# Block products with seven instead of eight multiplications: seven more pairs, one weight sum made earlier, and a new order inside a piece by eight

## The chip, the cores and the metric

The kernel runs on one core of a Trainium2 chip. The metric is device time in microseconds of one execution, as the median of several runs. Lower is better. PE is TensorE (matmul), DVE is VectorE, ACT is ScalarE, POOL is GpSimd, SP is SyncE, which here only issues DMAs.

## The reference, cut to what matters

One encoder layer for 256 tokens with 2048 features, all in float32:

```python
h = rms_norm(x, attn_norm)
qa, ka, va, qb, kb, vb, ga, gb = split(h @ w_in)
ya = windowed_gqa(qa, ka, va, table, sink_a)
yb = dilated_attention(qb, kb, vb, table)
merged = sigmoid(ga) * (ya @ w_branch_a) + sigmoid(gb) * (yb @ w_branch_b)
x = x + merged @ w_out
hf = rms_norm(x, ffn_norm)
g = dwconv_centred(hf @ w_ffn_gate, conv_w, conv_b)
x = x + (gelu(g) * (hf @ w_ffn_up)) @ w_ffn_down
x = x + sigmoid(rms_norm(x, ple_norm) @ w_ple_gate) * (p @ w_ple_proj)
out = rms_norm(x, final_norm)
```

Nearly all of the work is the product of 256 tokens with each weight matrix. What the change touches are the products of `ga` and `gb` (the gate columns of `w_in`), of `w_out`, and of the second half of `w_ffn_down`.

## The kernel before, in words

**Pieces.** The weights lie in memory as a list of pieces of 128 x 2048 floats, in the order in which they are used; `_pieces` makes the list. Each piece is loaded by SP into one of three buffers `raw`. A float32 product is made of three passes: ScalarE copies a stretch of `raw` to a rounded high half (`uh`, L305), VectorE subtracts it from the original for the low half (`ul`, L306), and TensorE multiplies high by high, high by low and low by high (`thirds`). A converted stretch is a unit. Units of plain weights go into a ring of six buffers (`u`), units that hold sums of weights into a ring of two (`v`, named `vh` and `vl`). A unit is made when a buffer of its ring is free, strictly in the order of the list (`produce`, `pump`, `drop`).

**Pairs by eight and by seven.** In the stages that `quads` describes, a piece is a pair: two chunks of 128 input features for two blocks of 512 output columns. With the two halves of the 256 tokens these are 2 x 2 x 2 = 8 block products, each three matmuls of 512 columns. A letter says how the pair is multiplied. "s" makes the eight products. "S" and "Z" make seven, after Strassen and Winograd, from sums of weight blocks and sums of activation blocks. The sums of activations (`combine`, `sums_of`) are made once for a pair of chunks and used by all stages that share these activations. For "S" VectorE makes the weight sums in `raw` by three subtractions (L295 to L297: 1024, 512 and 512 columns). For "Z" one sum is made earlier and lies in memory, so two subtractions are left (L282, L283: 512 and 1024 columns), and `load` takes that quarter of the piece from there (L255). Either kind converts four units: 512 columns and 1024 of plain weights, and 1024 and 1024 of sums.

**Sums made earlier.** `sum_ahead` makes the early sum of a "Z" pair in two parts: POOL loads 128 x 3 x 256 floats (L268), VectorE makes two subtractions or additions of 256 columns (L271, L272), POOL stores 128 x 256 floats (L275). These steps use `keep`, so they stay in the order in which they are written. Before the change this is done only in the two gate and up stages of the MLP, one part a job, in two small buffers (`act2`, `S4`) in turn; with `LASTS` = 30, from job 30 on only at every second job.

**Stages.** A: the projections for attention, one head's columns a job (16 chunks), with the heads' attention laid in between: scores on PE, softmax on VectorE and ScalarE, transposes on PE, values on PE, each at an entry of the table `due` (`at`, `run_due`). `hb` holds the position biases. B0 to B3: a quarter of the columns of both gates, eight pairs each, and after each the two branch products (ba, bb), which are plain. D0, D1: the output projection, eight pairs each, 1024 columns. E0: gate and up for half of the MLP; F00, F01: the down projection of this half, eleven pairs each. E1, F10, F11: the same for the other half. Then pp0, pp1 and G0 to G3 for the last block. The patterns of letters are `ALT`, `FIRST_GATES` and `DOWN` (L95 to L99). The order of the work on each engine is set by the order in which the code is written together with a scheduler that may bring an instruction forward.

**Order in a piece by eight.** In `quad_stage` the eight products of an "s" pair run over token half, column block and chunk, the chunk innermost (`t, n, c = g // 4, g // 2 % 2, g % 2`), and both units are dropped at the end of the pair.

Of the kernel before, what the change touches and what calls it, by code (L numbers as in the profile page):

```python
# [112 lines left out]
def _pieces():  # L113
# [44 lines left out]
    quads("G0", ("w_ple_gate", 0), ("w_ple_gate", WIDE), ALT.replace("S", "Z"))  # L158
# [35 lines left out]
def _encoder(ctx: ExitStack, tc, xt, pt, xrow, cols, gainrow, table, onehot, mask, ident_in, wts, out):  # L194
# [89 lines left out]

    def produce():

        u = state["unit"]
        p, kind, a, b = _UNITS[u]
        while state["raw"] < min(p + 3, _NPIECES):
            load(state["raw"])  # L290
        raw = raws[p]
        ring = "u" if kind == "n" else "v"
        if kind == "T13":
            q = [raw[:, i * WIDE:(i + 1) * WIDE] for i in range(4)]
            nc.vector.tensor_tensor(raw[:, :2 * WIDE], raw[:, WIDE:3 * WIDE], raw[:, :2 * WIDE], op=ALU.subtract)  # L295
            nc.vector.tensor_tensor(q[2], q[2], q[0], op=ALU.subtract)
            nc.vector.tensor_tensor(q[3], q[3], q[2], op=ALU.subtract)  # L297
# [7 lines left out]
        nc.scalar.activation(hi, src, AF.Copy)  # L305
        nc.vector.tensor_tensor(lo, src, hi.bitcast(F32), op=ALU.subtract)  # L306
# [108 lines left out]
    def quad_stage(stage, moving, combos=None, tags=("M2", "M3", "M4", "P22")):  # L415
# [24 lines left out]
        for i, p in enumerate(pieces):  # L440
# [407 lines left out]

    for i, job in enumerate(_JOBS):
# [60 lines left out]
    def sums_of(u, tag, s=None):  # L910
# [8 lines left out]
        if s is None:  # L919
            s = tok.tile([P, 2, 4, P], FR, name="S", tag="S%d" % tag)  # L920
# [387 lines left out]
```

## Time and profile before

| | |
|---|---|
| median of 3 runs | 1455.45 us (1454.93 to 1456.0) |
| span of the profiled execution | 1453.7 us, 1.75 us under the median |
| instructions | 19747 |
| busy PE / DVE / ACT / POOL | 1442.7 / 1220.8 / 829.6 / 73.8 us |
| share of the chain that ended last | PE 98% |
| conversions on VectorE (L306) | 519 and 96 |
| mean DMA rate | 213 GB/s |
| stage A from 60 us / B0 / D0 / D1 / E0 | to 304.2 / from 304.2 / 541.7 / 583.7 / 627.5 us |
| stage E1 / F10 / F11 | from 986.8 / 1231.7 / 1288.1 us, F11 to 1346.0 |

The profile shows one execution. A row of the timeline gives start, length, engine, line, operation and, in brackets, the idle time before it with what ended it. Lengths overlap: an instruction may start before the one ahead of it on its engine has ended, so what an instruction costs in a full engine is the distance between two starts. A window's row gives the busy time of each engine in that stretch, with overlaps counted once.

### The profile page before, as it was taken

How to read it: one execution, taken by the hardware profiler on the slowest of the kernel's cores; microseconds unless marked ns; L12 is line 12 of the kernel's file. 1: busy time of each engine (PE TensorE's matmuls, PEld its weight loads, DVE VectorE, ACT ScalarE, POOL GpSimd, SP SyncE). 2: the span in 40 equal slices, each digit the busy share in tenths (PEclk: the TensorE clock that was granted, in tenths of full speed). 3: DMA queues.
4: the chain of work that ended last, by engine and by line, in shares of the span. 5: the costliest groups of instructions: out<-in, count | busy, mean ns of one | idle time of the engine just before them, and what ended most of it. 6: DMA issues, size and time to landing. Idle time of an engine off the chain costs nothing.

```text
span 1453.7 us, 19747 instructions
## 1 busy us (share of the span) xinstructions
PE 1442.7 (99%) x7470; PEld 1234.0 (85%) x7470; DVE 1220.8 (84%) x1730; ACT 829.6 (57%) x1148; POOL 73.8 (5%) x113
## 2 busy tenths in 40 slices
PE   9999999999999999999999999999999999999997
PEld 8888888888888888888888888888888888888885
DVE  7677665679998989989877999997878799998994
ACT  7455544546555656566545566465545466555753
POOL 0000000000000000000221100000121200000000
PEclk9999999999999999999999999999999999999998
DMA  9753445435456456465767655566776765556462
GB/s 330 252 209 146 155 167 175 172 143 203 189 190 231 180 210 239 178 253 203 277 238 267 241 208 198 189 248 227 263 275 243 271 236 213 197 194 233 173 236 82
DMA packets 58522, 310.17 MB, mean 213 GB/s; under 512 B 7028, under 2 KB 12020, under 8 KB 29500
## 3 DMA queue, kind: packets, MB, share of 16 engines
q1 hardware_dynamic: 49388, 280.46, 53.1%
q0 software_dynamic: 8320, 27.27, 5.2%
q8 instruction: 58, 0.95, 0.3%
q10 hardware_dynamic: 720, 1.19, 0.2%
q14 instruction: 36, 0.29, 0.1%
HBM read 299.94 MB, written 8.95 MB: 212 GB/s over the span
## 4 chain that ended last, share of the span: by engine, by line
PE 98%; DMA 0%; issue 0%; DVE 0%; ACT 0%; SPq 0%; POOLq 0%; POOL 0%; DVEq 0%
PE bank L351 29%; PE bank L358 15%; PE bank L408 15%; PE bank L409 14%; PE bank L410 14%; PE bank L397 2%; PE bank L399 2%; PE bank L398 2%; PE bank L335 2%; PE bank L336 1%; PE bank L939 1%; PE bank L755 0%; PE bank L703 0%; PE bank L702 0%; PE bank L701 0%; DMA raw<-in_wts 0%
## 5 line engine op out<-in xcount | busy, mean ns | idle before, releaser
L305 ACT ACTIVATE uh<-raw 128x1024 fp32r<-128x1024 f32 (+2 forms) x519 | 518.1, 1010 | 297.0 <-PE bank L410 106.5
L306 DVE TENSOR_TENSOR ul<-raw,uh 128x1024 fp32r<-128x1024 f32 (+2 forms) x519 | 594.4, 1164 | 96.5 <-ACT uh L305 65.9
L351 PE MATMUL bank<-hf,uh 128*128 128x512 f32 x1408 | 336.3, 391 | 0.0
L351 PEld LDWEIGHTS bank<-hf,uh 128*128 128x128 f32 x1408 | 258.9, 188 | 50.1
L358 PEld LDWEIGHTS bank<-hf,ul 128*128 128x128 f32 x1408 | 180.4, 191 | 6.7
L358 PE MATMUL bank<-hf,ul 128*128 128x256 f32 x1408 | 182.8, 283 | 0.0
L305 ACT ACTIVATE vh<-raw 128x1024 fp32r<-128x1024 f32 x96 | 101.1, 1058 | 59.8 <-DVE raw L282 27.0
L306 DVE TENSOR_TENSOR vl<-raw,vh 128x1024 fp32r<-128x1024 f32 x96 | 116.3, 1220 | 1.1
L351 PE MATMUL bank<-hs,uh 128*128 128x512 f32 x432 | 103.6, 392 | 0.0
L351 PEld LDWEIGHTS bank<-hs,uh 128*128 128x128 f32 x432 | 79.5, 188 | 15.6
L410 PE MATMUL bank<-uh,act 128*128 128x512 f32 x218 | 84.9, 390 | 0.0
L409 PE MATMUL bank<-ul,act 128*128 128x512 f32 x218 | 84.8, 389 | 0.0
L408 PE MATMUL bank<-uh,act 128*128 128x512 f32 x218 | 84.6, 390 | 0.0
L496 ACT ACTIVATE t<-bank 128x256 f32<-128x256 f32 x122 | 45.3, 374 | 59.8 <-PE bank L358 48.7
L408 PE MATMUL bank<-uh,hs 128*128 128x512 f32 x172 | 67.4, 392 | 0.0
L410 PE MATMUL bank<-uh,hs 128*128 128x512 f32 x172 | 67.2, 391 | 0.0
L409 PE MATMUL bank<-ul,hs 128*128 128x512 f32 x172 | 67.0, 389 | 0.0
L1084 ACT ACTIVATE gw<-gw,cl 128x256 f32<-128x256 f32 x44 | 24.0, 594 | 72.2 <-DVE gw L1081 71.9
L271 DVE TENSOR_TENSOR ahead<-ahead 128x256 f32<-128x256 f32 x52 | 21.9, 422 | 46.8 <-DMA ahead<-in_wts 46.8
L268 POOL DMA_DIRECT2D ahead<-in_wts x52 | 39.0, 750 | 375.7 <-DMA ahead<-ahead 207.0
L358 PE MATMUL bank<-hs,ul 128*128 128x256 f32 x432 | 56.6, 284 | 0.0
L358 PEld LDWEIGHTS bank<-hs,ul 128*128 128x128 f32 x432 | 54.5, 191 | 1.0
(266 smaller groups left out, 2423.8 us busy)
## 6 DMA issues: line engine op xcount, KB each, us to landing
raw<-in_wts SPq DMA_DIRECT2D x225, 1024.0 KB, 4.9
ahead<-in_wts POOLq DMA_DIRECT2D x52, 384.0 KB, 5.2
raw<-in_wts SPq DMA_DIRECT2D x26, 768.0 KB, 5.1
ahead<-ahead POOLq DMA_DIRECT2D x52, 128.0 KB, 4.4
raw<-ahead SPq DMA_DIRECT2D x26, 256.0 KB, 4.9
raw<-in_wts SPq DMA_DIRECT2D x12, 512.0 KB, 7.0
xr<-in_xrow SPq DMA_DIRECT2D x4, 512.0 KB, 8.4
x<-in_xt SPq DMA_DIRECT2D x13, 128.0 KB, 6.0
```

What stands on the lines that cost most here:

```text
L268: keep(nc.gpsimd.dma_start(q, wts[p][:, :3 * WIDE].rearrange("p (q c) -> p q c", c=WIDE)[:, :, cols]))
L305: nc.scalar.activation(hi, src, AF.Copy)
L306: nc.vector.tensor_tensor(lo, src, hi.bitcast(F32), op=ALU.subtract)
L335: nc.tensor.matmul(acc, hi[:, w], m, start=first, stop=False, skip_group_check=True)
L351: nc.tensor.matmul(acc, weights(u)[0][:, o * P:(o + 1) * P], m, start=first, stop=False, skip_group_check=True)
L358: nc.tensor.matmul(acc[:, T:], weights(u)[1][:, o * P:(o + 1) * P], m[:, :T], start=False, stop=last, skip_group_check=True)
L397: nc.tensor.matmul(acc[:, :n * P], xh, hi, start=(k == 0), stop=False)
L398: nc.tensor.matmul(acc[:, :n * P], xh, lo, start=False, stop=False)
L408: nc.tensor.matmul(acc, sh, wh, start=first, stop=False)
L409: nc.tensor.matmul(acc, sh, wl, start=False, stop=False)
L410: nc.tensor.matmul(acc, sl, wh, start=False, stop=last)
L496: keep(nc.scalar.activation(t, acc[:, T:], AF.Copy, scale=scale))
```

## The change

Seven more pairs are multiplied by seven products: one in each of B1, B2, B3, D0, D1, F10 and F11. In B1 to D1 most sevens become "Z", whose early sum is made during stage A: 21 pairs in two parts, 42 sums, one at each of the slots that A's jobs offer (a quarter of a job for the wide value jobs), in two buffers behind the biases in `hb`. The part asked for at one slot is added two chunks after the next slot and then stored. The second half of the MLP has twelve "Z" pairs in F10 and F11 instead of ten, so its stage E1 makes 32 sums instead of 28. Combinations of activations are made for five pairs of `hs` instead of four, and for pairs 0, 2, 3, 5 and 6 of `merged` instead of 0, 2, 4 and 6. Where two pairs by seven follow each other, the sums of the second are now made behind its second unit for "S" too. In a piece by eight, except the last of its stage, the chunk is now the outermost of the three loops, and each unit is dropped when its four products are done.

```diff
-ALT = "SsSsSsSs"
-DOWN = ("ZZsZsZsZsZs", "ZsZsZsZsZss")
+ALT = "ZsZsZsZs"
+GATES = ("sssssSSs", "ZsZZsSZs", "ZsZZsSZs", "ZsZSsSZs")
+OUTS = "ZsZZsZZs"
+DOWN = ("ZZsZsZsZsZs", "ZZsZsZsZsZs")
-FIRST_GATES = "ssssSsSs"
...
-        behind = _PIECES[p][0] == "Z" == _PIECES[p - 1][0]
+        behind = _PIECES[p][0] in "SZ" and _PIECES[p - 1][0] in "SZ"
+        if kind == "T13" and not behind:
+            all_sums_of_weights(raw)
...
         if behind and u == _UNITS_OF[p][1]:
-            sums_of_weights(raw)
+            (sums_of_weights if _PIECES[p][0] == "Z" else all_sums_of_weights)(raw)
...
+                final = i == len(pieces) - 1
                 for g in range(8):
                     run_due(stage, i, g)
-                    t, n, c = g // 4, g // 2 % 2, g % 2
+                    t, n, c = (g // 4, g // 2 % 2, g % 2) if final else (g // 2 % 2, g % 2, g // 4)
                     w = cut(us[c], n if c == 0 else 1 - n)
                     put(tags[2 * t + n], part((a, b)[c], t), w)
-                drop(us[0])
-                drop(us[1])
+                    if not final and g % 4 == 3:
+                        drop(us[c])
+                if final:
+                    drop(us[0])
+                    drop(us[1])
...
-    hb = big.tile([P, QH * AW + BH * BW], F32, name="hb", tag="R1")
+    hb = big.tile([P, 2 * D * 2], F32, name="hb", tag="R1")
+    spare = [view(hb, QH * AW + BH * BW + e * 3 * T, (T, 3), (1, T)) for e in range(2)]
...
+    todo = [(p, h) for stage in ("B1", "B2", "B3", "D0", "D1") for p in _STAGES[stage] if _PIECES[p][0] == "Z"
+            for h in range(2)]
+    slots = [(i, k) for i in range(FIRST + 1, NA + 4)
+             for k in (range(0, KC, 16 // len(_JOBS[i][1])) if i < NA and _JOBS[i][0] == "v" else (0,))]
+    def asked(e):
+        add, store = sum_ahead(*todo[e], spare[e % 2])
+        i, k = slots[e + 1]
+        at((i, k + 2), add)
+        at((i, k + 3), store)
+
+    for e in range(len(todo)):
+        at(slots[e], asked, e)
...
-    for i, when in ((4, (3, 1)), (6, (3, 6)), (0, (5, 2)), (2, (7, 2))):
-        at(("B0", *when), combine, "hs", hs, i, i // 2)
+    for i, when, tag in ((5, (3, 6), 2), (6, (4, 5), 3), (0, (5, 5), 0), (2, (6, 5), 1), (3, (7, 2), 5)):
+        at(("B0", *when), combine, "hs", hs, i, tag)
...
-            at(("B3", 4, 4), combine, "merged", held["merged"], 4, 1)
+            at(("B3", 4, 4), combine, "merged", held["merged"], 3, 1)
+            at(("B3", 7, 4), combine, "merged", held["merged"], 5, 5)
```

The stage lists take `GATES[j]` for B0 to B3 and `OUTS` for D0 and D1; G0 keeps its pattern.

What moves on VectorE in stage A, between the softmax of one head (`den`, `rd`, the scaling of `s`) and that of the next (`s<-bank,hb`, `mx`). Before:

```order
L739 TENSOR_TENSOR den<-den,es 128x2
L500 TENSOR_TENSOR u<-bank,t 128x256
L741 RECIPROCAL rd<-den 128x2
L824 TENSOR_TENSOR u<-u,rms 128x256
L743 TENSOR_SCALAR s<-s,rd 128x256 x2
L508 TENSOR_TENSOR kf<-u,kf 128x256
L715 TENSOR_TENSOR s<-bank,hb 128x512
L781 TENSOR_TENSOR ya<-bank,ya 128x256
L726 TENSOR_REDUCE mx<-s 128x2
```

And a little later in the same run of jobs, with the change:

```order
L749 TENSOR_TENSOR den<-den,es 128x2
L509 TENSOR_TENSOR u<-bank,t 128x256
L751 RECIPROCAL rd<-den 128x2
L848 TENSOR_TENSOR k<-u,rms 128x128x2
L753 TENSOR_SCALAR s<-s,rd 128x256 x2
L272 TENSOR_TENSOR hb<-hb 128x256
L273 TENSOR_TENSOR hb<-hb 128x256
L791 TENSOR_TENSOR ya<-bank,ya 128x256
L725 TENSOR_TENSOR s<-bank,hb 128x512
```

The two operations of an early sum (`hb<-hb`) stand between two heads, ahead of the next head's scores; the first of them waits for the sum's load.

What moves on VectorE at the start of B2, where `c` and `merged` are the outputs of the quarter before, `raw<-raw` the sums of weights, `ul` and `vl` the conversions. Before, with "S" and "s" in turn:

```order
L295 TENSOR_TENSOR raw<-raw 128x1024
L306 TENSOR_TENSOR ul<-raw,uh 128x1024
L296 TENSOR_TENSOR raw<-raw 128x512
L306 TENSOR_TENSOR vl<-raw,vh 128x1024
L297 TENSOR_TENSOR raw<-raw 128x512
L943 SCALAR_TENSOR_TENSOR merged<-bank,merged 128x2x256
L306 TENSOR_TENSOR ul<-raw,uh 128x1024
L306 TENSOR_TENSOR vl<-raw,vh 128x1024
L943 SCALAR_TENSOR_TENSOR merged<-bank,merged 128x2x256
```

With the change ("Z", "s", "Z", "Z"):

```order
L283 TENSOR_TENSOR raw<-raw 128x512
L284 TENSOR_TENSOR raw<-raw 128x1024
L311 TENSOR_TENSOR ul<-raw,uh 128x512
L311 TENSOR_TENSOR vl<-raw,vh 128x1024
L968 SCALAR_TENSOR_TENSOR merged<-bank,merged 128x2x256
L311 TENSOR_TENSOR vl<-raw,vh 128x1024
L311 TENSOR_TENSOR ul<-raw,uh 128x1024
L283 TENSOR_TENSOR raw<-raw 128x512
L284 TENSOR_TENSOR raw<-raw 128x1024
L968 SCALAR_TENSOR_TENSOR merged<-bank,merged 128x2x256
```

Two sums of weights stand in front of a pair's conversions instead of three, and the sums of the next pair by seven follow within the same few rows, between the conversions of the first.

More of the change, by code (lines that the diff above doesn't have):

```diff
@@ L138, in _pieces @@
     for j in range(4):
-        quads("B%d" % j, ("w_in", GA * P + j * WIDE), ("w_in", GB * P + j * WIDE), ALT if j else FIRST_GATES)
+        quads("B%d" % j, ("w_in", GA * P + j * WIDE), ("w_in", GB * P + j * WIDE), GATES[j])
         wide("ba%d" % j, ("w_branch_a", j * WIDE), QH)
@@ L142, in _pieces @@
     for s in range(2):
-        quads("D%d" % s, ("w_out", 2 * s * WIDE), ("w_out", (2 * s + 1) * WIDE), ALT)
+        quads("D%d" % s, ("w_out", 2 * s * WIDE), ("w_out", (2 * s + 1) * WIDE), OUTS)
     for half in range(2):
@@ L157, in _pieces @@
         pieces.append(("s", [(n0, 0), (n1, 0), (n1, 1), (n0, 1)]))
-    quads("G0", ("w_ple_gate", 0), ("w_ple_gate", WIDE), ALT.replace("S", "Z"))
+    quads("G0", ("w_ple_gate", 0), ("w_ple_gate", WIDE), ALT)
     for s in (2, 3):
@@ L283, in sums_of_weights, with all_sums_of_weights @@
         nc.vector.tensor_tensor(raw[:, 2 * WIDE:], raw[:, 2 * WIDE:], view(q[0], 0, (0, 2), (1, WIDE)), op=ALU.subtract)
+    def all_sums_of_weights(raw):
+        q = [raw[:, i * WIDE:(i + 1) * WIDE] for i in range(4)]
+        nc.vector.tensor_tensor(raw[:, :2 * WIDE], raw[:, WIDE:3 * WIDE], raw[:, :2 * WIDE], op=ALU.subtract)
+        nc.vector.tensor_tensor(q[2], q[2], q[0], op=ALU.subtract)
+        nc.vector.tensor_tensor(q[3], q[3], q[2], op=ALU.subtract)
     def produce():
@@ L292, in produce @@
         ring = "u" if kind == "n" else "v"
[L293 to L297, printed above, removed]
-        behind = _PIECES[p][0] == "Z" == _PIECES[p - 1][0]
+        behind = _PIECES[p][0] in "SZ" and _PIECES[p - 1][0] in "SZ"
+        if kind == "T13" and not behind:
+            all_sums_of_weights(raw)
         if kind == "T21" and not behind:
@@ L674, in _encoder @@
     nc.sync.dma_start(hold, rows)
-    hb = big.tile([P, QH * AW + BH * BW], F32, name="hb", tag="R1")
+    hb = big.tile([P, 2 * D * 2], F32, name="hb", tag="R1")
+    spare = [view(hb, QH * AW + BH * BW + e * 3 * T, (T, 3), (1, T)) for e in range(2)]
     hba = hb[:, :QH * AW].rearrange("p (h c) -> p h c", c=AW)
-    hbb = hb[:, QH * AW:].rearrange("p (h c) -> p h c", c=BW)
+    hbb = hb[:, QH * AW:QH * AW + BH * BW].rearrange("p (h c) -> p h c", c=BW)
     def bias(h0, n):
@@ L847, in after @@
             attend(i, [(QH + g * HG + j, KVH + g * HG + j) for g in range(NG)], QH + j)
+    todo = [(p, h) for stage in ("B1", "B2", "B3", "D0", "D1") for p in _STAGES[stage] if _PIECES[p][0] == "Z"
+            for h in range(2)]
+    slots = [(i, k) for i in range(FIRST + 1, NA + 4)
+             for k in (range(0, KC, 16 // len(_JOBS[i][1])) if i < NA and _JOBS[i][0] == "v" else (0,))]
+    assert len(todo) < len(slots), (len(todo), len(slots))
+    def asked(e):
[5 more added lines that the diff above has]
+        at(slots[e], asked, e)
     for i, job in enumerate(_JOBS):
@@ L919, in sums_of @@
         if s is None:
-            s = tok.tile([P, 2, 4, P], FR, name="S", tag="S%d" % tag)
+            s = tok.tile([P, 2, 4, P], FR, name="S", tag="S%d" % tag if tag < 5 else "act2")
         nc.scalar.activation(s[:, 0], f, AF.Copy)
```

## The prediction

> **What bounds the kernel now.** I read the page first, then the chain of waits, the busy time by stage, and the timeline where a stage looked full.
>
> ```profile
> PE 1442.7 (99%) x7470; PEld 1234.0 (85%) x7470; DVE 1220.8 (84%) x1730; ACT 829.6 (57%) x1148; POOL 73.8 (5%) x113
> PE 98%; DMA 0%; issue 0%; DVE 0%; ACT 0%; SPq 0%; POOLq 0%; POOL 0%; DVEq 0%
> ```
>
> TensorE (PE) is the bound: the chain is 98% PE and nobody else holds it. A busy share of pipelined matmuls proves little by itself, so I took their spacing, in stage D1.
>
> ```profile
> 603.10 0.39 PE L409 MATMUL bank<-ul,merged 128*128 128x512 f32 x1
> 603.33 0.39 PE L410 MATMUL bank<-uh,merged 128*128 128x512 f32 x1
> 603.56 0.39 PE L408 MATMUL bank<-uh,merged 128*128 128x512 f32 x1
> 603.78 0.39 PE L409 MATMUL bank<-ul,merged 128*128 128x512 f32 x1
> ```
>
> A 512-wide matmul starts every 0.228 us, not every 0.39. At that pace the stages leave almost nothing over, so a matmul less is time less, if its operands are there. VectorE (DVE) makes the low halves of the weights and the sums of the sevens. Its spacing, again from start to start:
>
> ```profile
> 433.36 1.22 DVE L306 TENSOR_TENSOR ul<-raw,uh 128x1024 fp32r<-128x1024 f32 x1
> 434.49 1.22 DVE L306 TENSOR_TENSOR vl<-raw,vh 128x1024 fp32r<-128x1024 f32 x1
> 435.62 0.68 DVE L943 SCALAR_TENSOR_TENSOR merged<-bank,merged 128x512 fp32r<-128x512 f32 x1
> 436.22 0.68 DVE L931 TENSOR_TENSOR pair<-merged 128x512 f32<-128x512 f32 x1
> 436.82 0.69 DVE L306 TENSOR_TENSOR ul<-raw,uh 128x512 fp32r<-128x512 f32 x1
> 437.42 0.28 DVE L915 TENSOR_TENSOR cmb<-pair 128x128 f32<-128x128 f32 x1
> 437.63 1.22 DVE L295 TENSOR_TENSOR raw<-raw 128x1024 f32<-128x1024 f32 x1
> ```
>
> So 1024 columns cost 1.13 us, 512 cost 0.60 and 128 cost 0.20. By stage (columns: length, then busy time of PE, PEld, DVE, ACT, POOL, then clock, DMA share, GB/s):
>
> ```profile
> 60.00:304.20 244.20, 244.20 (x1389) 215.08 (x1389) 164.72 (x259) 128.55 (x208) 0.00 (x0) 1.00 0.50 180
> 304.20:627.50 323.30, 323.30 (x1460) 265.62 (x1459) 303.32 (x376) 189.77 (x220) 0.00 (x0) 1.00 0.54 197
> 541.70:583.70 42.00, 42.00 (x190) 34.38 (x188) 40.74 (x50) 25.73 (x28) 0.00 (x0) 1.00 0.68 247
> 583.70:627.50 43.80, 43.80 (x197) 34.95 (x196) 42.08 (x52) 26.80 (x35) 0.00 (x0) 1.00 0.53 200
> 986.80:1231.70 244.90, 244.90 (x1410) 216.48 (x1409) 204.30 (x331) 136.64 (x201) 37.03 (x56) 1.00 0.69 245
> 1231.70:1288.10 56.40, 56.40 (x251) 46.73 (x250) 51.40 (x58) 31.99 (x37) 0.00 (x0) 1.00 0.56 205
> 1288.10:1346.00 57.90, 57.90 (x262) 47.79 (x261) 54.07 (x68) 34.58 (x44) 0.00 (x0) 1.00 0.59 219
> ```
>
> The first row is stage A, the second B0 to D1, then D0, D1, E1, F10, F11. In A VectorE has a third of its time free; from B0 to D1 it has 20.0 us of 323.3 free, in D0 1.3, in D1 1.7. The saving must come out of stages in which the second engine is nearly full.
>
> **The change part by part.** *Products saved.* Seven pairs go from eight products to seven, one each in B1, B2, B3, D0, D1, F10, F11. A product is three 512-wide matmuls: 7 x 3 x 0.228 = 4.8 us off PE, 0.685 a stage. PE holds the chain, so all of it counts while no operand is late.
>
> *VectorE from B0 to D1.* A pair by eight costs two conversions, 2.27 us. "S" costs three sums and 512 + 3 x 1024 columns of conversion, 2.33 + 4.00 = 6.3. "Z", whose fourth sum is made earlier, costs two sums, 1.73 + 4.00 = 5.7. B1 and B2 go from 4 S + 4 s (34.4) to 4 Z + S + 3 s (36.1), +1.7 each; B3 to 3 Z + 2 S + 3 s, +2.2; D0 and D1 to 5 Z + 3 s, +1.1 each: +7.8. Two more combinations of activations at 0.60 + 4 x 0.20 + 0.60 = 2.0 add 4.0; about three of the 42 advance sums fall behind 304.2, 2.0. VectorE then has 303.3 + 13.8 = 317.1 us of work, and PE 323.3 - 5 x 0.685 = 319.9. Of 20.0 us of idle time 2.8 are left. It can be idle against its will (a buffer not yet free, a high half not yet made), so the loss is 317.1 + 20.0 f - 319.9, with f the part of the old idle time that is forced: nothing up to f = 0.14, 17.2 us at f = 1. How much is forced is seen where VectorE is already the tighter one, in D1:
>
> ```profile
> 583.70:588.00 4.30, 4.30 (x20) 3.56 (x19) 4.30 (x8) 2.36 (x4) 0.00 (x0) 1.00 0.94 389
> 596.00:600.00 4.00, 4.00 (x21) 3.28 (x20) 4.00 (x6) 2.17 (x4) 0.00 (x0) 1.00 0.23 51
> 604.00:608.00 4.00, 4.00 (x19) 2.67 (x17) 3.46 (x5) 4.00 (x6) 0.00 (x0) 1.00 0.22 94
> ```
>
> It runs full there at both ends of the first 16 us, so most idle time can be filled when work is waiting; around 605 it is idle with PE at its heels. I take f = 0.25, 2.2 us, nearest to these rows, nearly all in D1, which starts with VectorE further behind by D0's +1.1 and the shorter PE time. The new order of a piece by eight (first unit free after four products) hands a buffer back 2.7 us sooner and costs no matmul; I count it at nothing, covered by the ring (0 to -0.5).
>
> *Sums in A.* 39 sums of two 256-wide subtractions (0.67 us a sum, below) put 26 us on VectorE in A: 164.7 becomes 191 of 244.2. The weights' path runs many microseconds ahead; softmax doesn't, and each head's chain is in VectorE's queue behind a sum that waits for its DMA. The chain's slack, writer above reader:
>
> ```profile
> 111.81 0.68 DVE L760 TENSOR_TENSOR near<-bank,near 128x512 fp32r<-128x512 f32 x1
> 113.38 0.28 PE L701 MATMUL bank<-near,v 128*128 128x256 f32 x1
> ...
> 180.11 0.88 DVE L743 TENSOR_SCALAR s<-s,rd 128x512 f32<-128x512 f32 x2
> 182.18 1.03 PE L755 MATMUL bank<-ident,s 128*128 128x128 f32 x8
> ```
>
> That is 0.9 and 1.2 us, so 0.67 fits and a late DMA doesn't. Whether the DMA is late, stage E of today shows, where the same loop of load, sum, store runs on two buffers (the timeline, then all waits of these sums, then those of E1):
>
> ```profile
> 694.78 0.75 POOL L268 DMA_DIRECT2D ahead<-in_wts  x1 [4.04 <-DMA ahead<-ahead]
> 700.15 0.43 DVE L271 TENSOR_TENSOR ahead<-ahead 128x256 f32<-128x256 f32 x1 [1.10 <-DMA ahead<-in_wts]
> 700.83 0.42 DVE L272 TENSOR_TENSOR ahead<-ahead 128x256 f32<-128x256 f32 x1
> 701.65 0.58 POOL L275 DMA_DIRECT2D ahead<-ahead  x1
> 706.30 0.74 POOL L268 DMA_DIRECT2D ahead<-in_wts  x1 [4.06 <-DMA ahead<-ahead]
> DVE ahead L271 <- DMA ahead<-in_wts: 46.8, 25, 3.3
> L271 DVE TENSOR_TENSOR ahead<-ahead x28: 411/424/430, 1010.5 to 1175.6; 128x256 f32<-128x256 f32 x28
> ```
>
> One buffer's turn takes 706.30 - 694.78 = 11.5 us, 5.8 a sum. In A 39 sums have 244.2 us, 6.3 each: it mostly fits. Bounds: 0, and 12 heads x (0.67 + a mean wait of 46.8 / 52 = 0.9, less 0.9) = 8 us. I take 0.4, near the low end, since the pace of A is the slower one. POOL has nothing else to do in A (0.00), and 42 x 512 KB add 90 GB/s to 180, below the 389 that the row of D1 reaches: the raw loads stay covered.
>
> *Four more sums in E1.* The last row above (the sums of E1 by their source line) has 28 sums, so 27 intervals of 165.1 / 27 = 6.1 us, against a job of PE of 5.57:
>
> ```profile
> 1120.50 3.65 PE bank L351 x16
> 1124.15 1.91 PE bank L358 x16
> 1126.07 3.65 PE bank L351 x16
> ...
> 1164.87 3.82 PE L351 MATMUL bank<-hf,uh 128*128 128x512 f32 x16
> 1165.17 1.04 ACT L305 ACTIVATE uh<-raw 128x1024 fp32r<-128x1024 f32 x1
> ```
>
> VectorE and ScalarE so fall behind by 0.54 us a sum. When the sums end, the second unit of the job at 1164.87 is ready at 1166.21, and PE needs it 8 x 0.228 later, at 1166.70: 0.5 us of cover is left. The change goes on with four sums, one in two jobs and all in one buffer, whose turn of 11.5 us stands against 11.1: about 0.4 us more lag each, 1.5 in all, less the 0.5. I take 0.6 (0 to 1.5). The Trainium skill's page "DMA: Bandwidth & Descriptors" (section "Anatomy of one DMA") gives such a DMA about 2.0 us plus its bytes at 436 GB/s. By that the turn would be some 7 us, an estimate, there would be no lag, and this term would be zero; the trace's 46.8 us of waits speak against it.
>
> *F10 and F11.* Two pairs go from s to Z, +3.5 us a stage: 54.9 of 55.7 and 57.5 of 57.2. F11 is over by 0.3 and G0 follows at once: 0.4 (0 to 1.5).
>
> Sum against the profiled span of 1453.7: -4.8 + 2.2 + 0.4 + 0.6 + 0.4 = -1.2. The median of the runs is 1455.45, 1.75 us above that span, for what lies around it, which does not change: **1454.2 us**. A measurement tells about 0.2%, 2.9 us, so this is no change that can be told.
>
> **The rivals.** *Everything is saved.* VectorE's idle time is free to use (f up to 0.14), the sums stay hidden: 1455.45 - 4.8 = 1450.7, up to 1452.5 with 1.8 us of small losses. For it: D1's full rows, and the chain without any DVE share. Against it: D1 starts with no reserve, and E1's cover of 0.5.
>
> *VectorE becomes the bound from B1 to D1.* The sums of the sevens have only two buffers ("v"), and the new patterns put sevens side by side (positions 2-3 and 5-6), so the second must wait for the first one's buffer and idle time is forced. Place: B1 to D1; price 20 us a unit of f; it decides from f = 0.45, where the loss of 6.2 and the other 1.4 eat the saving and 2.9 more. At f = 0.5: 7.2 - 4.8 + 1.4 = +3.8, 1459.2. For it: 2.8 us of reserve in 320, and the 3.46 of 4.00 at 604. Against it: F00 and F01 open with two Z side by side today and lose nothing on the chain.
>
> *The products aren't saved* is excluded: the order holds 21 fewer matmuls of 512.
>
> **How the numbers follow.** Forecast 0.45, all saved 0.37, VectorE the bound (or A's chains near their upper bound) 0.18. The forecast's own range, with A, E1 and F11 between their bounds near the taken values, is 1452.5 to 1457. Going out to the rivals, 1450.7 to 1459.2 leaves out little below and some 0.1 above. Faster by over 0.2% is the first rival, 0.37; slower by over 0.2% the second, 0.18; the rest 0.45.
>
> **What would show it.** Right: 21 matmuls fewer; DVE busy over 97% from B1 to D1; matmul gaps of 0.1 to 0.5 us in D1's first 20 us and near the last sums of E1; B1 and B2 shorter by about 0.7 each. Wrong: no gap in D1 (all saved), or gaps behind the side-by-side sevens in B1 and B2, or PE waiting for "near" or "s" in A, each with a DVE row that waits for the DMA of a sum ahead of it.

## The result, and the profile after

The change makes the kernel slower, by about half a percent. Its median is 1462.56 us of 7 executions (1460.25 to 1473.2) beside 1455.28 us for the kernel before (1454.88 to 1456.0): a ratio of 1.0063, 95% interval 1.0046 to 1.0080. The forecast was 1454.2 in a range up to 1459.2, so the time lies 3.4 us above the range. The executions also spread over 13 us, where those of the kernel before stay within 1.1. (The quotient of the two medians is 1.0050; the ratio given is near that of the two means, which the long executions raise.)

The profiled execution took 1460.34 us with a span of 1458.1, 4.4 more than the span before. It is one of the three shortest of the seven, so the profile accounts for 4.4 us and not for all of the loss of the median, 7.3. Its page, busy times and the engines' shares of the chain:

```profile
PE 1441.5 (99%) x7449; PEld 1230.7 (84%) x7449; DVE 1269.1 (87%) x1852; ACT 837.5 (57%) x1166; POOL 134.7 (9%) x205
PE 87%; DVE 6%; issue 3%; DMA 3%; ACT 1%; POOL 0%; SPq 0%; POOLq 0%; DVEq 0%
```

The 21 matmuls are gone (7470 to 7449). But the chain that was 98% PE is now 87% PE; most of the rest is VectorE, DMAs and issue. A share of the chain is not a loss: 13% of the span is far more than the 4.4 us lost. But it says that there are now places where TensorE waits. Where they lie, by the first matmul of each stage:

| stretch | before, us | after, us | difference |
|---|---|---|---|
| to the end of A | 304.2 | 304.2 | 0 |
| B0 with its branch products | 62.7 | 68.3 | +5.6 |
| B1 to D1 | 260.6 | 256.8 | -3.8 |
| E0, F00, F01 | 359.2 | 359.4 | +0.2 |
| E1 | 244.9 | 244.9 | 0 |
| F10 | 56.5 | 58.4 | +1.9 |
| F11 to the end | 165.6 | 166.0 | +0.5 |

The same stretches as in the prediction, by the windows of the profile after: A, B1 to D1 as a whole, D0, D1, E1, F10 (length, then busy time of PE, PEld, DVE, ACT, POOL, granted clock, DMA share, GB/s):

```profile
60.00:304.20 244.20, 244.20 (x1389) 215.05 (x1388) 190.53 (x334) 128.42 (x208) 49.66 (x75) 1.00 0.73 260
372.50:629.30 256.80, 256.78 (x1150) 210.61 (x1149) 253.47 (x306) 159.25 (x187) 0.00 (x0) 1.00 0.57 209
545.00:586.20 41.20, 41.20 (x186) 33.86 (x186) 40.92 (x48) 26.14 (x30) 0.00 (x0) 1.00 0.69 247
586.20:629.30 43.10, 43.08 (x194) 34.56 (x193) 43.01 (x54) 27.59 (x37) 0.00 (x0) 1.00 0.53 192
988.80:1233.70 244.90, 244.90 (x1410) 216.47 (x1409) 205.34 (x339) 136.97 (x200) 42.33 (x64) 1.00 0.71 253
1233.70:1292.10 58.40, 56.62 (x249) 45.93 (x248) 55.70 (x66) 33.08 (x41) 0.00 (x0) 1.00 0.57 211
```

VectorE is busy 253.47 of 256.8 us from B1 to D1, 99%, and PE is busy 256.78: the five products of these stages are saved in full (5 x 0.685 = 3.4). In A VectorE has 25.8 us more to do (164.72 to 190.53) and nothing is lost. The loss is at the start of B0 and in F10. From F11 to the end a product is saved and yet 0.5 us more are needed, so about a microsecond is lost there too, in gaps of some 0.3 us and less.

**The start of B0.** TensorE in the timeline after:

```profile
306.06 0.39 PE L415 MATMUL bank<-uh,hs 128*128 128x512 f32 x1
309.94 0.80 PE L413 MATMUL bank<-uh,hs 128*128 128x512 f32 x1 [3.49 <-DVE u L511]
310.53 0.63 PE L414 MATMUL bank<-ul,hs 128*128 128x512 f32 x1
310.95 0.63 PE L415 MATMUL bank<-uh,hs 128*128 128x512 f32 x1
311.38 0.42 PE L711 MATMUL bank<-kf,qf 128*128 128x256 f32 x1
...
313.73 0.48 PE L413 MATMUL bank<-uh,hs 128*128 128x512 f32 x1
```

The matmul that should start at 306.29 starts at 309.94. It opens the bank (a buffer in which TensorE adds up products until they are read) that the last projection of A has filled, and it was released by L511, VectorE's reading of that projection. What VectorE did before it, and POOL's DMAs for the early sums (load L269, store L276):

```profile
301.24 0.42 DVE L272 TENSOR_TENSOR hb<-hb 128x256 f32<-128x256 f32 x1
301.69 0.42 DVE L273 TENSOR_TENSOR hb<-hb 128x256 f32<-128x256 f32 x1
306.85 0.42 DVE L272 TENSOR_TENSOR hb<-hb 128x256 f32<-128x256 f32 x1 [4.73 <-DMA hb<-in_wts]
307.20 2.35 DVE L311 TENSOR_TENSOR ul<-raw,uh 128x1024 fp32r<-128x1024 f32 x2
309.47 0.42 DVE L511 SCALAR_TENSOR_TENSOR u<-bank,t 128x256 f32<-128x256 f32 x1
```

```profile
298.53 0.59 POOL L276 DMA_DIRECT2D ahead<-hb  x1 [1.89 <-DVE hb L273]
301.58 0.74 POOL L269 DMA_DIRECT2D hb<-in_wts  x1 [2.46 <-DMA ahead<-hb]
```

The load at 301.58 had to wait for the landing of a store (the bracket of its row). It landed 5.2 us after it was issued, and VectorE's addition followed at 306.85. VectorE had reached the addition at 302.1 and stood there 4.73 us, with two conversions and the reading of the bank queued behind. In the kernel before, the same reading was at 305.81 and the bank was opened at 308.51 (rows below). Two parts of the change meet here. In the order of the code an addition of A stands behind the first half of the next job's matmuls, some 9 us after its load was asked for (a job of 5.57 and 16 x 0.228); in B0 the same entry of the table comes behind the first product, some 3 us sooner. And with the chunk outermost, a piece opens its third bank with its third product (the fourth in the order of the trace) and not with its fifth.

The stall has a second price. The windows around it:

```profile
306.30:309.90 3.60, 0.15 (x1) 0.00 (x0) 3.05 (x5) 0.00 (x0) 0.74 (x1) 0.98 0.26 94
309.90:313.70 3.80, 3.76 (x17) 3.49 (x17) 1.65 (x4) 1.06 (x1) 0.59 (x1) 0.57 0.74 287
313.70:318.00 4.30, 4.30 (x22) 3.55 (x21) 3.21 (x6) 1.22 (x2) 0.74 (x1) 1.00 0.12 43
```

The granted clock (the share of TensorE's full clock) is 0.57 on average in the 3.8 us behind the gap. The 17 matmuls from 309.94 to 313.73 take 3.79 us; the same 17 took 2.21 in the kernel before (two rows of its TensorE, and below them its VectorE's reading of the bank):

```profile
306.30 0.39 PE L408 MATMUL bank<-uh,hs 128*128 128x512 f32 x1
...
308.51 0.47 PE L408 MATMUL bank<-uh,hs 128*128 128x512 f32 x1
```

```profile
305.81 0.42 DVE L502 SCALAR_TENSOR_TENSOR u<-bank,t 128x256 f32<-128x256 f32 x1
```

So 3.65 us of waiting and 1.6 us of slow clock make most of the 5.6.

**F10.** The second gap, in the first pair of F10, and VectorE's last readings of E1's banks:

```profile
1236.87 0.39 PE L415 MATMUL bank<-vh,ends 128*128 128x512 f32 x1
1238.78 0.47 PE L413 MATMUL bank<-uh,ends 128*128 128x512 f32 x1 [1.52 <-DVE pair L509]
```

```profile
1238.21 0.75 DVE L509 TENSOR_TENSOR pair<-bank,t 128x256 f32<-128x256 f32 x2
```

F10 needs as its sixth bank one that E1 has filled, and VectorE reads it only at 1238.5, 4.9 us after F10's first matmul at 1233.67. Before, it did so 3.1 us after, just in time (VectorE's last reading, and F10's first matmul):

```profile
1234.73 0.42 DVE L500 TENSOR_TENSOR pair<-bank,t 128x256 f32<-128x256 f32 x1
```

```profile
1231.67 0.40 PE L408 MATMUL bank<-uh,ends 128*128 128x512 f32 x1
```

So VectorE ends E1 later than it did.

### The profile page after: what moved, and what is told of

Same layout as the page of the kernel before. It is cut to its first block, busy times and chain, and to the rows that moved or that the text cites. A ratio compares the mean times of both kernels' runs of the same rounds, so it can differ in the third digit from the quotient of the medians.

```text
span 1458.1 us, 20096 instructions
## 1 busy us (share of the span) xinstructions
PE 1441.5 (99%) x7449; PEld 1230.7 (84%) x7449; DVE 1269.1 (87%) x1852; ACT 837.5 (57%) x1166; POOL 134.7 (9%) x205
## 4 chain that ended last, share of the span: by engine, by line
PE 87%; DVE 6%; issue 3%; DMA 3%; ACT 1%; POOL 0%; SPq 0%; POOLq 0%; DVEq 0%
PE bank L356 23%; PE bank L414 14%; PE bank L413 13%; PE bank L415 13%; PE bank L363 12%; PE bank L402 2%; PE bank L404 2%; PE bank L403 2%; DVE ul L311 2%; PE bank L340 2%; DMA ahead<-in_wts 2%; PE bank L341 1%; PE bank L964 1%; DMA ahead<-ahead 1%; PE bank L765 0%
## 5 line engine op out<-in xcount | busy, mean ns | idle before, releaser
L310 ACT ACTIVATE uh<-raw 128x1024 fp32r<-128x1024 f32 (+2 forms) x519 | 512.0, 1004 | 271.1 <-PE bank L356 82.6
L310 ACT ACTIVATE vh<-raw 128x1024 fp32r<-128x1024 f32 x110 | 115.2, 1055 | 73.1 <-DVE raw L283 41.4
L311 DVE TENSOR_TENSOR vl<-raw,vh 128x1024 fp32r<-128x1024 f32 x110 | 132.6, 1220 | 2.3 <-ACT vh L310 1.0
L414 PE MATMUL bank<-ul,act 128*128 128x512 f32 x208 | 81.0, 390 | 0.0
L415 PE MATMUL bank<-uh,act 128*128 128x512 f32 x208 | 81.0, 389 | 0.0
L413 PE MATMUL bank<-uh,act 128*128 128x512 f32 x208 | 80.6, 389 | 0.0
L269 POOL DMA_DIRECT2D ahead<-in_wts x56 | 41.9, 748 | 391.3 <-DMA ahead<-ahead 221.8
L413 PE MATMUL bank<-uh,hs 128*128 128x512 f32 x154 | 61.1, 396 | 3.5 <-DVE u L511 3.5
L415 PE MATMUL bank<-uh,hs 128*128 128x512 f32 x154 | 60.4, 392 | 0.0
L414 PE MATMUL bank<-ul,hs 128*128 128x512 f32 x154 | 60.3, 392 | 0.0
L284 DVE TENSOR_TENSOR raw<-raw 128x1024 f32<-128x1024 f32 x49 | 59.8, 1220 | 0.1
```

Of the source, the lines that this page charges most:

```text
L269: keep(nc.gpsimd.dma_start(q, wts[p][:, :3 * WIDE].rearrange("p (q c) -> p q c", c=WIDE)[:, :, cols]))
L284: nc.vector.tensor_tensor(raw[:, 2 * WIDE:], raw[:, 2 * WIDE:], view(q[0], 0, (0, 2), (1, WIDE)), op=ALU.subtract)
L413: nc.tensor.matmul(acc, sh, wh, start=first, stop=False)
L414: nc.tensor.matmul(acc, sh, wl, start=False, stop=False)
L415: nc.tensor.matmul(acc, sl, wh, start=False, stop=last)
```

## The experiments

Theory 1: two costs that the prediction lacks, the wait for a sum's load where A passes into B0, and VectorE's lag at the end of E1. Rival: the prediction's own, a VectorE too full from B1 to D1. For F10 a rival is the order of the instructions at the border of E1 and F10. The kernels below ran in groups of four (*s_in_down* and *three_more_again* in a group of two); each group shares a chip and the executions of the kernel before, whose medians there are 1455.3 to 1455.8 us.

**again**: the changed kernel once more, nothing edited.

> The changed kernel once more. In the first profile VectorE stands 4.7 us at 302 us before an early sum whose load has not landed; a projection's result lies behind it, TensorE waits 3.65 us for that bank, and then runs for 3.8 us at a granted clock of 0.57. Theory 'the sum's load at the border of A and B0': the wait depends on when a DMA lands, so the times spread over 1460 to 1473 again, the median is near 1462, and the profile shows the same gap at 306 us with another length, and in slow executions more than one such gap. Theory 'VectorE too full from B1 to D1': the excess over the before kernel lies in gaps between 372 and 629 us, in the same place each time.

Measured: 1465.10 us (1463.69 to 1468.32), ratio 1.0068, 1.0055 to 1.0081. The gap at 306 us is there (4.1 us, at 305.9), none is new between 372 and 629, and F10 loses 5.8 us instead of 2.6. F10's gap and the clock behind it:

```profile
1243.33 0.47 PE L413 MATMUL bank<-uh,ends 128*128 128x512 f32 x1 [3.35 <-DVE pair L509]
```

```profile
1239.50:1243.30 3.80, 0.47 (x3) 0.05 (x2) 3.80 (x11) 1.93 (x5) 0.00 (x0) 1.00 0.28 111
1243.30:1247.20 3.90, 3.87 (x12) 3.05 (x12) 3.87 (x6) 3.65 (x5) 0.00 (x0) 0.65 0.00 0
```

The places are the same in these two executions, the lengths are not, and F10's loss differs more than B0's gap.

**late_adds**: the additions that fall into B0 come eight steps later.

```diff
-        at((i, k + 2), add)
-        at((i, k + 3), store)
+        d = 8 if i >= NA else 0
+        at((i, k + 2 + d), add)
+        at((i, k + 3 + d), store)
```

> Only the sums whose addition falls into B0 are added and stored eight steps later; nothing else changes. Theory 'the sum's load at the border': the gap of 3.65 us at 306 us and the 1.9 us at low clock behind it go, so the time falls by about 5.5 to some 1455 to 1457, and the spread from run to run shrinks to about 1 us. Theory 'VectorE too full from B1 to D1': no change, 1460 to 1463.

Measured: 1461.77 (1461.26 to 1463.56), ratio 1.0046, 1.0034 to 1.0058; 3.3 us less than *again*. The gap at 306 is gone and so is the low clock. But 2.3 us come back in B0's second pair by seven. VectorE now waits for the load of one of these sums 20 us later, and the last addition stands at 332.6 and 333.6 among the sums and conversions of the two S pairs (VectorE's wait, then TensorE's):

```profile
325.80 0.42 DVE L272 TENSOR_TENSOR hb<-hb 128x256 f32<-128x256 f32 x1 [2.54 <-DMA hb<-in_wts]
```

```profile
341.25 0.51 PE L413 MATMUL bank<-vh,S 128*128 128x512 f32 x1 [0.41 <-ACT S L947]
342.86 0.50 PE L414 MATMUL bank<-vl,S 128*128 128x512 f32 x1 [1.10 <-DVE vl L311]
```

The cause of the first gap holds, the gain was put too high: moving these sums moves a part of their cost. That the 2.3 us come from these additions is argued from their place, and not shown by a run.

**old_order**: the pieces by eight in the old order.

```diff
-                final = i == len(pieces) - 1
+                final = True
```

> The pieces by eight run in the old order (chunk innermost, both units dropped at the end); the rest of the change stays. At the start of B0 the third bank is then opened by the seventh instead of the fourth product, about 2.2 us later. Theory 'the sum's load at the border': the gap shrinks from 3.65 to about 1.4 us or goes, and with it the low clock, so about 4 us less, 1456 to 1459, unless the later return of buffers costs VectorE something from B1 to D1, where it is busy 98.7% in the changed kernel: then up to 3 us come back there. Theory 'VectorE too full from B1 to D1': slower than the changed kernel, 1463 or more, with new gaps only between 372 and 629 us.

Measured: 1463.33 (1458.86 to 1468.23), ratio 1.0053, 1.0036 to 1.0069: not told apart from *again*. VectorE waits for the same load (4.47 us, to 306.01). TensorE now meets it at the next thing behind it, the scaled `q` of the last scores, and 2.24 us later than its turn:

```profile
309.94 0.71 PE L730 MATMUL bank<-k,q 128*128 128x128 f32 x4 [2.24 <-DVE q L848]
```

In this order the third bank is opened by the fifth product (not by the seventh, as the expectation has it). So the order of products only decides who waits first. The clock stays at 1.00 behind this shorter gap. What is saved in B0 is lost in F10 of the profiled execution, the longest of the six (9.0 us), and E1 loses 3.3.

**s_for_z**: all Z of B1 to D1 become S; no early sums in A.

```diff
-GATES = ("sssssSSs", "ZsZZsSZs", "ZsZZsSZs", "ZsZSsSZs")
-OUTS = "ZsZZsZZs"
+GATES = ("sssssSSs", "SsSSsSSs", "SsSSsSSs", "SsSSsSSs")
+OUTS = "SsSSsSSs"
```

> Every Z pair of B1 to D1 becomes an S pair: the same products by seven, no early sums in A, but a third subtraction for each of 21 pairs on VectorE, 0.6 us each, 12.6 us in all. Theory 'the sum's load at the border': no gap at 306 us, so 5.5 us less there; VectorE is asked for 253.5 + 12.6 = 266 us in the 256.8 us of B1 to D1, so TensorE now loses about 9 us there, spread over the sevens: 1463 to 1466 in all. If VectorE's idle time were partly forced (the forecast's f of 0.25 on an idle time of 20 us), the loss would be 5 us larger.

Measured: 1473.14 (1469.85 to 1475.87), ratio 1.0119, 1.0106 to 1.0133. No gap at 306 us. The added work isn't lost evenly: B1 to B3 lose next to nothing, D0 and D1 nearly all of it.

```profile
372.00:545.00 173.00, 173.00 (x770) 140.64 (x769) 170.57 (x209) 104.37 (x120) 0.00 (x0) 1.00 0.52 194
545.00:650.00 105.00, 98.10 (x440) 77.42 (x438) 102.31 (x123) 61.33 (x78) 0.00 (x0) 0.97 0.55 205
```

By the spacing of the matmuls some 12 us more are lost between 550 and 650 us than before, for 12.6 us of added work. So VectorE has next to nothing to spare, and the place where a lack shows is late, as the prediction had it. It just wasn't lacking in the change. The total is some 8 us above the expected: these 12 us were put at 9, and most of the rest is F10, which loses 8.4 us in this profile instead of 2.6.

**old_ends**: as many pairs by seven in F10 and F11, but first and last pairs as before.

```diff
-DOWN = ("ZZsZsZsZsZs", "ZZsZsZsZsZs")
+DOWN = ("ZZsZsZsZsZs", "ZsZZsZsZZss")
```

> In the second half of the MLP the pattern is ZsZZsZsZZss instead of ZZsZsZsZsZs: as many pairs by seven and as many early sums, but it begins and ends as the pattern before the change does. In two profiles of the changed kernel TensorE waits 1.7 and 3.5 us in the first two pairs of F10 for a bank whose reading by VectorE stands behind the sums of the second Z pair and behind the activation sums of pair 9; in the order of this kernel both stand elsewhere, as before the change. Theory 'order at the border of E1 and F10': the loss in F10 falls from 2.6 to 6 us to under 0.5, so 2.5 to 5 us less than the changed kernel. Theory 'the four more sums make VectorE late in E1': only the part of the order goes, about 1 us of it, and 2 us or more of the wait in F10 stay and vary from run to run.

Measured: 1463.72 (1460.22 to 1465.31), ratio 1.0048, 1.0033 to 1.0063. F10 loses 2.8 us in the profiled execution, the fastest of the six. The theory of the order falls: with the old order at the border TensorE still waits for VectorE's readings of E1's banks.

**old_down**: the second half of the MLP has the old pattern, `ZsZsZsZsZss`; all else as in the change.

> The second half of the MLP has the old pattern, ten Z pairs and 28 sums; everything before it stays as in the change. Both theories of F10 expect no loss there: of the change's seven products five are left (-3.4 us), the gap with slow clock at the start of B0 stays (5.5 to 7), so 1457.4 to 1459 against 1455.3 before, and less spread than the changed kernel. If the loss in F10 came from something earlier in the kernel, it stays and the time is 1460 or more.

Measured: 1457.88 (1455.95 to 1460.22), ratio 1.0015, 1.0006 to 1.0024. No loss in F10; the gap at the start of B0 is there (3.84 us). So both are separate, and what was changed for F10 and F11 costs some 5 to 7 us net (1462.6 and 1465.1 on other chips, less 1457.9).

**down_only**: the kernel before with only the new pattern for F10 and F11.

> The kernel before with only the new pattern for the second half of the MLP: two products by seven more in F10 and F11, four more early sums in E1. The prediction's terms for this part were -1.4 + 0.6 + 0.4 = -0.4, so 1454.9. The theories of F10 expect -1.4 + 2.6 to 6 + 1 (G0 and the stages ahead of it), so 1457.5 to 1461, with a spread of some us, and a gap in the first two pairs of F10.

Measured: 1466.78 (1465.55 to 1467.94), ratio 1.0073, 1.0060 to 1.0086. This part alone, put at -0.4 in the prediction, costs 11.5 us on this chip, more than any theory said. In its profile F10 loses 8.9 us. Why this part costs more alone than within the change isn't shown.

**sums_end_in_a**: the old pattern in the MLP, and three Z to S, so that the 36 sums end inside A.

```diff
-GATES = ("sssssSSs", "ZsZZsSZs", "ZsZZsSZs", "ZsZSsSZs")
-OUTS = "ZsZZsZZs"
-DOWN = ("ZZsZsZsZsZs", "ZZsZsZsZsZs")
+GATES = ("sssssSSs", "ZsZZsSZs", "ZsZZsSZs", "ZsZSsSSs")
+OUTS = "ZsZSsZZs"
+DOWN = ("ZZsZsZsZsZs", "ZsZsZsZsZss")
```

> The old pattern in the second half of the MLP, and three Z pairs of B3, D0 and D1 turned into S: 36 early sums, so the last is added and stored inside A, and no VectorE instruction of B0 waits for one. Five products more by seven stay (-3.4 us). Theory 'the sum's load at the border': no gap at 306 us and no low clock; VectorE gets 3 x 0.6 us more work from B1 to D1, 255.3 us in 256.8, which costs 0 to 2 us: 1452 to 1454, a spread of 1 us, and so faster than the kernel before. If sums in A cost TensorE time anywhere else, or VectorE's fullness does, it is 1455 or more.

Measured: 1455.65 (1454.07 to 1459.89), ratio 0.9999, 0.9988 to 1.0010, where 1452 to 1454 was expected. No gap at the start of B0, but now D1 loses, with VectorE busy without a break and units made too late:

```profile
590.00:606.00 16.00, 14.74 (x70) 11.27 (x69) 16.00 (x21) 10.37 (x16) 0.00 (x0) 1.00 0.31 101
```

D0 and D1 take 86.1 us (539.0 to 625.1) against 85.8 before, though two products are saved in them: 1.8 us of added VectorE work, in stages that were 99% full, cost about as much. The profiled execution, one of the longest of the twelve, lost 5.8 us in E1 besides. How much of such a loss is in the median wasn't traced.

**sums_later**: the kernel before, its 28 sums of E1 at jobs 9 to 36 instead of 2 to 29.

```diff
-LASTS = 30
+LASTS = 37
...
-            if i > 1 and todo and (i % 2 == 0 or i < LASTS):
+            if (i > 8 or i > 1 and not half) and todo and (i % 2 == 0 or i < LASTS):
```

> The kernel before, with its own patterns; only the 28 early sums of E1 run at jobs 9 to 36 instead of 2 to 29, one a job as before. In the profiles VectorE falls behind TensorE by about half a microsecond with each sum (17 us at job 30 of the kernel before), works that off when the sums are over, and is 3.2 us behind at the end, just in time for F10. In the changed kernel the sums end at job 37 and it is 5.0 and 7.5 us behind in two executions, which lost 2.6 and 5.8 us in F10. Theory 'the sums of E1 end too late': with the sums ending at job 37 and nothing else changed, VectorE is 5 to 10 us behind at the end and F10 loses 2 to 8 us: 1457 to 1464. Theory 'order at the border of E1 and F10': the order there is that of before, so no loss: 1455.3.

Measured: 1465.01 (1464.86 to 1467.88), ratio 1.0065, 1.0052 to 1.0079. The same products, patterns and number of sums, the same order at the border, and 9.3 us more than the before of its own runs (1455.74). The first matmul of F10 is at 1231.63 as before; VectorE's last reading is 7.7 us later than before:

```profile
1242.47 0.42 DVE L500 TENSOR_TENSOR pair<-bank,t 128x256 f32<-128x256 f32 x1
```

```profile
1234.29 0.47 PE L408 MATMUL bank<-vh,S 128*128 128x512 f32 x1 [1.80 <-ACT vh L305]
1240.97 0.76 PE L408 MATMUL bank<-uh,ends 128*128 128x512 f32 x1 [2.88 <-DVE pair L500]
```

**lasts34**: the changed kernel, `LASTS = 34`, so its 32 sums run at jobs 2 to 33.

> The changed kernel, with the 32 sums of E1 at every job from 2 to 33, so that they end at job 34 instead of 37; the order at the border of E1 and F10 stays. Theory 'the sums of E1 end too late': VectorE is 3 to 5 us behind at the end instead of 5 to 7.5, and F10 loses 0 to 2.5 us instead of 2.6 to 6, so some 3 us less than the changed kernel's 1462.6 to 1465; the lag before that peaks higher, and where it passes about 19 us E1 itself loses up to 4 us. Theory 'order at the border': no change in F10.

Measured: 1463.63 (1460.37 to 1464.5), ratio 1.0046, 1.0033 to 1.0059. A miss: VectorE is 6.9 us behind at the end, not 3 to 5, and F10 loses 4.5. This lies between the two executions of the changed kernel (5.0 and 7.5), so ending three jobs sooner wins nothing that these profiles show.

The lag of all profiles together, worked out from the traces: start of VectorE's last reading of a bank of E1, less the start of E1's last matmul. Beside it the loss in F10: what the distances of its matmuls exceed 0.23 us (0.12 for 256 columns), summed over 56 us; the slow clock behind a gap is part of it.

| kernel | sums in E1 | lag, us | loss in F10, us |
|---|---|---|---|
| sums_end_in_a | 28 | 2.1 | 0 |
| three_more, and again | 28 | 2.8, 3.5 | 0, 0 |
| order_only | 28 | 2.9 | 0 |
| before | 28 | 3.2 | 0 |
| old_down | 28 | 3.3 | 0 |
| s_in_down | 28 | 3.3 | 0.8 |
| changed kernel | 32 | 5.0 | 2.6 |
| old_ends | 32 | 5.6 | 2.8 |
| lasts34 | 32 | 6.9 | 4.5 |
| again (changed kernel) | 32 | 7.5 | 5.8 |
| late_adds | 32 | 7.7 | 6.0 |
| old_order | 32 | 9.4 | 9.0 |
| down_only | 32 | 10.6 | 8.9 |
| s_for_z | 32 | 10.8 | 8.4 |
| sums_later | 28, later | 11.0 | 9.5 |

Up to 3.5 us nothing is lost (the 0.8 of *s_in_down*, below, lies in the middle of the stage); beyond it the loss grows by about one microsecond with each microsecond of lag. In the kernel before, the same lag taken job by job reaches 17.3 us at the 31st job and then falls, when the sums are over.

**three_more**: only the three products of B1 to B3 stay; D0 and D1 have four Z at the old places; the old pattern in the MLP; 36 sums.

```diff
-GATES = ("sssssSSs", "ZsZZsSZs", "ZsZZsSZs", "ZsZSsSZs")
-OUTS = "ZsZZsZZs"
-DOWN = ("ZZsZsZsZsZs", "ZZsZsZsZsZs")
+GATES = ("sssssSSs", "ZsZZsSZs", "ZsZZsSZs", "ZsZSsSSs")
+OUTS = "ZsZsZsZs"
+DOWN = ("ZZsZsZsZsZs", "ZsZsZsZsZss")
...
-            at(("B3", 4, 4), combine, "merged", held["merged"], 3, 1)
-            at(("B3", 7, 4), combine, "merged", held["merged"], 5, 5)
+            at(("B3", 4, 4), combine, "merged", held["merged"], 4, 1)
```

> Only three of the change's seven products are kept, those of B1 to B3. D0 and D1 go back to four pairs by seven, but Z instead of S, B3 has two Z, and the second half of the MLP has its old pattern: 36 early sums, all inside A. Theory 'every cost of the change is in the two late ends of sums and in a VectorE that is filled in D1': no gap at the start of B0, less work for VectorE in D0 and D1 than in the kernel before (5.7 instead of 6.3 us a pair), F10 as before. So 3 x 0.685 = 2.1 us less than before, and up to 0.4 us less in D1: 1452.8 to 1453.3. Theory 'sums in A or the new order cost time by themselves': 1455 or more.

Measured: 1452.58 (1451.67 to 1457.89), ratio 0.9976, 0.9967 to 0.9986, and a second time, as **three_more_again**, 1452.61 (1451.76 to 1457.31), ratio 0.9978, 0.9969 to 0.9987.

> The kernel with three of the change's products once more, on the same chip as the one above: 1452.6, with single executions up to 1458 where a sum's load in E1 comes late.

Faster than both kernels, by 3.2 us beside the before of its own runs (1455.74), a little more than expected: D0 and D1 take 84.9 us (539.9 to 624.8) against 85.8. The products count when no sum's wait reaches TensorE at the two borders. The chain is back at 98% PE, and D1 has VectorE with time to spare:

```profile
PE 98%; DMA 0%; issue 0%; ACT 0%; DVE 0%; SPq 0%; POOLq 0%; POOL 0%; DVEq 0%
```

```profile
579.00:622.00 43.00, 43.00 (x197) 35.10 (x196) 40.61 (x50) 26.84 (x35) 0.00 (x0) 1.00 0.51 192
```

**order_only**: the kernel before with the new order of the pieces by eight.

> The kernel before with only the new order of the products in a piece by eight. My prediction took it at 0 to -0.5 us, covered by the ring of buffers. If the earlier use of the third bank at the start of B0 costs by itself, TensorE has a gap there, up to 2 us; if the earlier return of buffers helps VectorE, D1 loses less than its 1.3 us. I expect 1454.8 to 1455.5.

Measured: 1455.68 (1454.37 to 1463.43), ratio 1.0003, 0.9991 to 1.0014. No difference, and no gap at the start of B0: the early third bank costs nothing while VectorE is on time.

**s_in_down**: *three_more* with the sixth pair by seven of F10 and F11 as S, without early sums.

```diff
-DOWN = ("ZZsZsZsZsZs", "ZsZsZsZsZss")
+DOWN = ("ZZsZsZsZsZs", "ZsZsZSZsZss")
...
-        seven = [i for i, c in enumerate(DOWN[half]) if c == "Z"]
+        seven = [i for i, c in enumerate(DOWN[half]) if c != "s"]
```

> The kernel with three of the change's products, and the two of F10 and F11 added in another way: the sixth pair by seven of each of these stages is an S pair in the middle (ZsZsZSZsZss), which needs no early sum, so E1 has its 28 sums as before. VectorE makes 6.3 instead of 2.3 us of weight work for that pair, and one more set of activation sums in E1. Theory 'the sums of E1 end too late': VectorE is about 3 us behind at the end of E1 as before, F10 loses nothing, and 2 x 0.685 = 1.4 us less than 1452.6 is left of the time, 1451.2 to 1452. Theory 'the pair itself is too much for VectorE in F10 and F11' (51.9 + 4.0 us of work in 55.6, 50.6 + 4.0 in 56.3): a loss of 1 us or more in F10, and no gain over 1452.6.

Measured: 1452.72 (1451.33 to 1455.17), ratio 0.9979, 0.9970 to 0.9988: no gain over *three_more*. VectorE ends E1 3.3 us behind, so the big loss is gone with the four sums. But F10 and F11 lose 2.0 us by the spacing of their matmuls where *three_more* loses 0.5 (0.6 the second time), which eats the 1.4 of the two products. Both theories were right in part: the early sums cost the several microseconds, the pair itself its own gain.

## Why the prediction was wrong, step by step

Two steps failed. The wait of an early sum where A passes into B0 was put at nothing and cost 5.6 us with the slow clock behind it. The lag that four more sums leave VectorE at the end of E1 was put at 0.6 us, inside E1, and cost 2.6 and 5.8 us in F10. Term by term:

- *Products saved, 4.8 us.* Right in kind and size: 3.4 of the 3.8 us by which B1 to D1 got shorter. The condition "while no operand is late" failed for F10 and F11.
- *VectorE from B0 to D1, 2.2 us lost, nearly all in D1.* No more was lost there than before: D0 and D1 take 84.3 us against 85.8, with two products less. The work was put too high: 13.8 us more forecast, 60.43 + 253.47 - 303.3 = 10.6 measured (the row of B0 is `304.20:372.50`, below). At f = 0.25 the prediction's own formula then gives 313.9 + 5.0 - 319.9 = -1.0, no loss. The edge was real and near: *sums_end_in_a* and *s_for_z* lose in D1 and D0.
- *Sums in A, 0.4 us.* None was lost in A. The step that failed stands a paragraph earlier: "about three of the 42 advance sums fall behind 304.2, 2.0" priced them by their work and not by their wait. I saw that "each head's chain is in VectorE's queue behind a sum that waits for its DMA", and looked for it in A, where additions come 9 us after their load was asked for; where the table of entries passes into B0 they come sooner. One wait of 4.7 us cost 5.6.
- *Four more sums in E1, 0.6 us (0 to 1.5).* The cause was named, the place and the size were not. E1 itself lost nothing. I counted the cover at job 30, where 0.5 us is left, and not what the lag does at the end: F10 reuses E1's banks after five products. The loss in F10 is 2.6 and 5.8 us in two executions of the changed kernel.
- *F10 and F11, 0.4 us (0 to 1.5).* Priced by VectorE's work alone; the lag it starts with was left out. *s_in_down* shows about the work's own price, 1.4 us (with S pairs, 4.0 us of work in place of 3.5); in the changed kernel about 1 us was lost from F11 on, within the range.
- *New order, 0 to -0.5.* Right alone (*order_only*).
- *Rivals.* VectorE did not become the bound from B1 to D1. Of the signs set down as "wrong", the last came closest: TensorE waits, with a DVE row that waits for a sum's DMA ahead of it. It just waits for another tile, one stage later. Of the signs of "right", the 21 matmuls, VectorE's 99% and the shorter B1 and B2 came true beside a wrong time: they test the products and VectorE's work, and not the waits.

The row of B0 for the second point:

```profile
304.20:372.50 68.30, 64.81 (x296) 53.56 (x295) 60.43 (x95) 35.30 (x45) 4.53 (x7) 0.98 0.48 175
```

The page "DMA: Bandwidth & Descriptors" of the Trainium skill (section "Anatomy of one DMA") gives a DMA about 2.0 us plus its bytes at 436 GB/s, so 2.9 us for the load of a sum, an estimate, by which E1 would have no lag. The runs differ: the load at 301.58 took 5.2 us, and moving the sums in E1 cost 9.3 us with nothing else changed.

What stays open: why the landing of these loads differs so much between executions that the lag of one and the same kernel ends at 5.0 or 7.5 us. Single executions of the kernel before take up to 1460.7 us too, and none of those was traced. It wasn't tried to free POOL's loads from the stores ahead of them with a third buffer.

## What to carry to other kernels

An operation whose input comes by DMA, put into the queue of an in-order engine, must be priced by what stands behind it when the DMA is late, and at each border of stages anew, since the same entry of a table lies at another distance there. Work that makes a second engine fall behind is not free because it ends within its stage: ask how many microseconds behind the engine is at the stage's end, and which bank or buffer the next stage needs first. When an addition to a nearly full engine loses, try a part of it: three of the seven products gain 3 us (0.9 of it in D0 and D1, which got less VectorE work) where all seven lose 7.

## What the runs showed of the hardware

A stall of TensorE can cost more than its length. Behind idle times of 3.49 us (changed kernel, 309.94) and 3.35 us (*again*, 1243.33) the granted clock was 0.57 and 0.65 on average over the next 3.8 and 3.9 us; behind 2.24 us (*old_order*) it stayed at 1.00:

```profile
307.40:310.00 2.60, 0.36 (x4) 0.17 (x2) 2.60 (x6) 0.00 (x0) 0.22 (x1) 1.00 0.61 176
310.00:314.00 4.00, 4.00 (x20) 3.40 (x21) 2.71 (x6) 1.26 (x2) 0.37 (x1) 1.00 0.69 279
```

The length of a stall alone doesn't decide it. Behind 1.88 us in E1 (*sums_end_in_a*, first two rows) the clock was 0.50 for 3.4 us, and behind 2.88 us in F10 (*sums_later*, 1240.97, last row) for 6.7 us:

```profile
1169.10 2.54 PE L356 MATMUL bank<-hf,uh 128*128 128x512 f32 x8 [1.88 <-ACT uh L310]
1170.60:1174.00 3.40, 3.40 (x15) 3.21 (x14) 3.40 (x7) 3.24 (x5) 1.03 (x2) 0.50 0.32 95
1240.90:1247.60 6.70, 6.27 (x14) 4.56 (x15) 6.70 (x10) 4.38 (x5) 0.00 (x0) 0.50 0.43 156
```

The Trainium skill's page "TensorE: Matmul & The Clock Gate" (section "Part 1: The HAM clock gate") says that the clock is halved after about 3.4 us without work and needs about as long a busy stretch to come back. The changed kernel's trace agrees with both (idle for 3.49 us, 0.57 over 3.8 us, then 1.00). The other runs agree only in part: the two of the last rows had the half clock behind shorter stalls, and *sums_later* had it for about twice as long.

VectorE was 99% busy over 257 us (253.47 of 256.8), and these stages lost no more TensorE time than in the kernel before; with 1.8 us more work (*sums_end_in_a*) D0 and D1 did lose.
